# The seam behind a scan: pools per k tile, a split operand stored in DRAM, and a second partial sum through DRAM

## The chip, the cores and the metric

The kernel runs on one core of a Trainium2 chip. The core has five engines that each work through their own queue in order: TensorE (PE in the profile; its weight loads are PEld), VectorE (DVE), ScalarE (ACT), GpSimd (POOL) and SyncE (SP). SP, ACT and POOL also issue transfers (their queues are SPq, ACTq, POOLq). The metric is device time in microseconds of one execution; the time before is the median of three runs, 2103.34 us (2099.37 to 2106.05).

## The reference

One layer of a streaming encoder, in float32, for 1024 frames of width 1024:

```
u = rms_norm(x, ln1) * (1 + scale1) + shift1          # shift, scale, gate from silu(c) @ w_ada
gl, cb, cc, cx, z, xbc, dt = split(u @ w_in)
p_conv = (cb * causal_conv3(cc * cx)) @ w_conv_out
xs, bs, cs = split(silu(causal_conv4(xbc) + bias))
y = ssd_scan(xs * dt, dt * a, bs, cs) + d_skip * xs   # 32 heads in 8 groups, state 128
y = group_rms_norm(y * silu(z)) * ssm_norm_w
p_ssm = y @ w_ssm_out
x = x + gate1 * ((sigmoid(gl1) * p_conv + sigmoid(gl2) * p_ssm) @ w_o)
u2 = rms_norm(x, ln2) * (1 + scale2) + shift2
x = x + gate2 * (relu(u2 @ w_up) ** 2 @ w_down)
out = rms_norm(x, final_norm)
```

## The kernel before

Everything is held feature-major: a tile has 128 features on the partitions and 1024 frames, in two halves of 512. A matrix product is done in float32r from split operands: each operand is a high part (a cast on ACT) and a low part (operand minus high part, on DVE), and three matmuls (high x high, high x low, low x high) of 128x512 make one step over 128 inputs (`mm3`, lines 118 to 123). `proj` (line 125) does eight such steps for one output tile. `strassen_pair` (line 145) makes two output tiles at once with seven products instead of eight; its `wsplit` makes the four weight operands wa, w12, w34 and wb, each a whi and a wlo from the pool `weights`, which holds four of each in turn. A tile that is asked for while its place is still read waits for the last reader.

The stages, in order: the norm that makes u (`uh`, `ul`: high and low parts of eight k tiles, one pool `u`); a small projection for dt; the branch gates gl; z (eight pairs); the conv branch (for f0 = 0, 2, 4, 6: a v pair for f0, a v pair for f0+1, a y pair for both); the xBC projections, group by group (two x tiles, B, C), with the scan of the group before woven in; then the seam, where u is no longer needed and the conv output projection `wco` starts, with the scan of the last group woven in; then the SSD output projection `wso` in four quarters b = 0 to 3 of four k tiles each, the projection `wo`, and the MLP.

What the change touches, in the kernel before:

- 32 gemvs (line 319, a DVE instruction each, over 128x1024 weights that POOL loads) make the columns of the later modulation. They use one buffer `wv` (line 572) and stand in the gl and z stages: 4 with each gl pair from f = 12 on, 3 with each z pair.
- The conv branch writes each finished y tile (`glt`) to DRAM (`yc_d`, one float32 tile, line 662, ACT's queue). At the seam SP loads it into `ccs` (line 850, three buffers), and ACT and DVE split it into `ys` (`split`, line 108), one of eight tiles of the pool `yy`, which takes the place of `u`.
- `xbc_tile` (line 707) takes its weights from `load_w_acc` (line 99): the high part by a cast, the low part as the raw weights times -1 on ACT, and then a transfer on POOL's queue that adds the raw weights in DRAM. It copies the projection from PSUM to a padded tile `raw` and makes the tap sum `cacc` from PSUM.
- In `wso`, quarter 0 copies its sums from PSUM to `gt` and stores them to DRAM (`s_d`); quarter 1 loads them into slots and adds; quarters 2 and 3 add on in the slots. `finish` (line 806) makes a group's sum of squares, and `rstd` (line 822) the reciprocal roots of four groups, through DRAM (`ssq_d`, `rst_d`); the y tiles of a quarter are loaded (`yr`, two buffers, on SP), multiplied by the broadcast roots (`rb`, one buffer) on DVE and split into `ys`. `finish` of the last group stands at quarter 0, f = 2, `rstd(1)` at quarter 0, f = 5; quarters 2 and 3 need its result.

The order on each engine is not the order of the text: a scheduler places the instructions by an estimate of their times, and the priority follows the text.

Of the kernel before, what the change touches and what calls it, by code (L numbers as in the profile page):

```python
# [8 lines left out]
F32 = mybir.dt.float32  # L9
# [29 lines left out]
def hybrid_trunk(tc, xT, par, hrows, crow, wada1, wadak, wada2, win, wdt, wco, wso, wo, wup, wdt_, wdn, out):  # L39
# [43 lines left out]
    yc_d = dp.tile([8, P, T], F32, name="yc_d")  # L83
# [170 lines left out]
    up = tc.alloc_tile_pool(name="u", bufs=1, side="right")  # L254
    uh = [[up.tile([P, H], F32R, name=f"uh{k}{h}") for h in (0, 1)] for k in range(KT)]
    ul = [[up.tile([P, H], F32R, name=f"ul{k}{h}") for h in (0, 1)] for k in range(KT)]
# [284 lines left out]
    p0d = tc.alloc_tile_pool(name="p0d", bufs=1, reuse_waits="tile")
    wdr = p0d.tile([P, KT, NH], F32, name="wdr")
# [19 lines left out]

    p0d.release()
# [3 lines left out]
    gem = iter(range(32))  # L567

    def gemvs(n):
        for _, i in zip(range(n), gem):  # L570
            w_ = pe1.tile([P, T + 32], F32, name="wv", bufs=1)[:, 0:T]
            pool.dma_start(w_, wada2[i])  # L572
            gemv(w_, 16 + i)

# [28 lines left out]
    for f in range(8, 16, 2):  # L603
        ts_ = [glp.tile([P, T], F32, name="glt") for _ in (0, 1)]

        def gl_ev(i, h, src):
            act.activation(ts_[i][:, hs[h]], src, AF.Tanh, scale=0.5)

        if f == 10:
            dt_chain()  # L610
        elif f > 10:
            gemvs(4)
        strassen_pair(pe1, win[f], win[f + 1], X, gl_ev)
        for i in (0, 1):
            act.dma_start(gl_d[f + i], ts_[i])
    for g in range(NG):
        ts_ = [glp.tile([P, T], F32, name="glt") for _ in (0, 1)]

        def z_ev(i, h, src):
            t = ts_[i][:, hs[h]]  # L620
            act.activation(t, src, AF.Tanh, scale=0.5)
            stt(t, t, 1.0, src, ALU.add, ALU.mult)

        gemvs(3)
        strassen_pair(pe1, win[gtile(g) + 4], win[gtile(g) + 5], X, z_ev)
        for i in (0, 1):
            act.dma_start(z_d[2 * g + i], ts_[i])
# [9 lines left out]
    for f0 in range(0, 8, 2):  # L637
# [23 lines left out]
        for i in (0, 1):  # L661
            act.dma_start(yc_d[f0 + i], ys_[i])
# [33 lines left out]
    pcf = tc.alloc_tile_pool(name="pcf", bufs=2, reuse_waits="tile")  # L696
# [4 lines left out]
    padded = [p2t.tile([P, T + 3], F32, name=f"raw{i}", bufs=1) for i in (0, 1)]  # L701
# [4 lines left out]
    def xbc_tile(win_i, ci, dst):  # L706
        ps = proj(load_w_acc(win[win_i]), uh, ul)
# [4 lines left out]
        for h in (0, 1):  # L712
            act.activation(a[:, hs[h]], ps[h], AF.Identity, bias=hb[:, ci:ci + 1], scale=hw[:, 4 * ci + 3:4 * ci + 4])  # L713
# [5 lines left out]
    def proj_group(g):  # L719
# [7 lines left out]
        xbc_tile(b + 2, 16 + g, bf)  # L727
        xbc_tile(b + 3, 24 + g, cf)
# [126 lines left out]
    pcf.release()  # L855
# [4 lines left out]
    for f in range(8):  # L860
        drive(gen)
        gt = gp.tile([P, T], F32, name="gt")
        sp.dma_start(gt, gl_d[f])
        ps = proj(load_w(wco[f]), ych, ycl)
        for h in (0, 1):
            stt(gt[:, hs[h]], gt[:, hs[h]], 1.0, ps[h], ALU.add, ALU.mult)
        act.dma_start(at_d[f], gt)
    prev = drive(gen)
# [5 lines left out]
    for b in range(4):  # L874
        yh, yl = [], []
        for k in range(4):
# [7 lines left out]
            ys = yy.tile([P, 2, T], F32R, name="ys")  # L884
# [3 lines left out]
        if b == 1:  # L888
# [4 lines left out]
        for f in range(8):  # L893
            if f % 2 == 0:
                w = load_w(wso[b, f // 2])
            if b == 0:
                if f == 2:
                    finish(prev, last_mm[0])
                if f == 5:
                    rstd(1)  # L900
                gt = gp.tile([P, T], F32, name="gt")
                ps = proj(w, yh, yl, nk=4, base=(f % 2) * 512)
                for h in (0, 1):
                    act.copy(gt[:, hs[h]], ps[h])
# [9 lines left out]
            for h in (0, 1):  # L914
                if b == 1:
# [18 lines left out]
    yy.release()  # L934
# [283 lines left out]
```

## Time and profile before

| | |
|---|---|
| median of three runs | 2103.34 us |
| profiled execution | 2105.2 us |
| its span, first to last instruction | 2103.4 us |
| mean granted TensorE clock | 0.992 |
| TensorE busy | 2072.5 us (99%) |
| VectorE busy | 1473.1 us (70%) |
| ScalarE busy | 963.0 us (46%) |
| GpSimd busy | 182.6 us (9%) |
| conv branch | about 371 to 597 us |
| seam: last scan product, first conv output matmul | 1061.69 us, 1066.10 us |

In a row of the timeline stand the start, the duration, the engine, the line of the kernel, the operation and `out<-in`, and in brackets the idle time of the engine before it and what ended that. In a row of the waits of TensorE stand the total, the number of times and the longest. In a row of the windows stand the length, then for PE, PEld, DVE, ACT and POOL the busy time and the number of instructions, then the granted clock, the share of DMA time and GB/s.

### The profile page before, as it was taken

How to read it: one execution, taken by the hardware profiler on the slowest of the kernel's cores; microseconds unless marked ns; L12 is line 12 of the kernel's file. 1: busy time of each engine (PE TensorE's matmuls, PEld its weight loads, DVE VectorE, ACT ScalarE, POOL GpSimd, SP SyncE). 2: the span in 40 equal slices, each digit the busy share in tenths (PEclk: the TensorE clock that was granted, in tenths of full speed). 3: DMA queues.
4: the chain of work that ended last, by engine and by line, in shares of the span. 5: the costliest groups of instructions: out<-in, count | busy, mean ns of one | idle time of the engine just before them, and what ended most of it. 6: DMA issues, size and time to landing. Idle time of an engine off the chain costs nothing.

```text
span 2103.4 us, 26276 instructions
## 1 busy us (share of the span) xinstructions
PE 2072.5 (99%) x9760; PEld 1698.4 (81%) x9760; DVE 1473.1 (70%) x2310; ACT 963.0 (46%) x1600; POOL 182.6 (9%) x251
## 2 busy tenths in 40 slices
PE   8999999999999999999999999999999999999997
PEld 6878877888888888887878788888888888888887
DVE  8757777776637778877796748745866665658775
ACT  4433232332246768676564531224554454544432
POOL 0000000000000000000000000012000001232213
PEclk8999999999999999999999999999999999999998
DMA  8315645222274555555366676453144347988932
GB/s 327 106 64 187 203 161 194 87 70 74 77 202 111 123 123 136 140 142 137 99 207 219 213 282 198 167 194 118 61 165 165 150 157 268 304 239 254 284 75 81
DMA packets 139666, 345.16 MB, mean 164 GB/s; under 512 B 13153, under 2 KB 48353, under 8 KB 138002
## 3 DMA queue, kind: packets, MB, share of 16 engines
q1 hardware_dynamic: 98258, 200.14, 29.8%
q0 software_dynamic: 27856, 107.49, 18.0%
q10 hardware_dynamic: 13424, 35.85, 4.4%
q8 instruction: 77, 1.26, 0.2%
q14 instruction: 51, 0.42, 0.1%
HBM read 270.88 MB, written 72.55 MB: 163 GB/s over the span
## 4 chain that ended last, share of the span: by engine, by line
PE 87%; issue 8%; DMA 2%; DVE 1%; POOL 1%; ACT 0%; SPq 0%; DVEq 0%; POOLq 0%; ACTq 0%
PE mm L154 25%; PE mm L121 13%; PE mm L123 13%; PE mm L120 13%; PE mm L1111 11%; PE B L761 2%; PE mm L398 2%; PE B L766 2%; PE C L783 1%; PE sx L398 1%; PE st L398 1%; DMA wraw<-in_win 1%; POOL wv L572 1%; PE A L738 1%; DMA x<-in_xT 1%
## 5 line engine op out<-in xcount | busy, mean ns | idle before, releaser
L154 PE MATMUL mm<-t,whi 128*128 128x512 f32 x1104 | 340.9, 391 | 4.6 <-DVE cq L44 4.6
L154 PEld LDWEIGHTS mm<-t,whi 128*128 128x128 f32 x1104 | 207.6, 188 | 49.7 <-DVE cq L44 6.7
L154 PE MATMUL mm<-t,wlo 128*128 128x512 f32 x552 | 214.9, 390 | 0.0
L1111 PE MATMUL mm<-op,whi 128*128 128x512 f32 x672 | 207.0, 389 | 0.0
L121 PE MATMUL mm<-ul,whi 128*128 128x512 f32 x512 | 203.7, 398 | 0.0
L120 PE MATMUL mm<-uh,whi 128*128 128x512 f32 x512 | 203.3, 397 | 0.0
L44 DVE TENSOR_TENSOR wlo<-s,whi 128x1024 fp32r<-128x1024 f32 (+1 forms) x124 | 124.0, 1012 | 63.5 <-ACT whi L159 62.6
L123 PE MATMUL mm<-uh,wlo 128*128 128x512 f32 x512 | 162.3, 395 | 0.0
L44 DVE TENSOR_TENSOR wlo<-wraw,whi 128x1024 fp32r<-128x1024 f32 (+1 forms) x132 | 141.1, 1069 | 22.8 <-ACT whi L94 16.1
L120 PE MATMUL mm<-ys,whi 128*128 128x512 f32 x384 | 148.5, 394 | 3.7 <-ACT ys L109 3.7
L121 PE MATMUL mm<-ys,whi 128*128 128x512 f32 x384 | 148.8, 394 | 0.6 <-DVE ys L44 0.6
L47 DVE SCALAR_TENSOR_TENSOR cacc<-raw,hw,cacc 128x1024 f32<-128x1024 f32 x96 | 122.8, 1279 | 37.7 <-ACT cacc L713 37.0
L1111 PEld LDWEIGHTS mm<-op,whi 128*128 128x128 f32 x672 | 126.1, 188 | 26.2
L154 PE MATMUL mm<-s,whi 128*128 128x512 f32 x448 | 138.0, 389 | 0.7 <-ACT cu L177 0.7
L159 ACT CAST whi<-wraw 128x1024 fp32r<-128x1024 f32 x76 | 63.5, 836 | 157.8 <-PE mm L154 128.5
L1111 PE MATMUL mm<-op,wlo 128*128 128x512 f32 x336 | 130.7, 389 | 0.0
L755 ACT ACTIVATE seg<-acb,acum 128x128 f32<-128x128 f32 x256 | 81.9, 395 | 106.6 <-PE B L761 101.5
L47 DVE SCALAR_TENSOR_TENSOR y<-mm,mcol,y 128x512 f32<-128x512 f32 (+1 forms) x100 | 69.3, 704 | 78.1 <-PE mm L1111 41.3
L94 ACT CAST whi<-wraw 128x1024 fp32r<-128x1024 f32 x52 | 54.6, 1052 | 149.2 <-PE mm L121 127.0
L123 PE MATMUL mm<-ys,wlo 128*128 128x512 f32 x384 | 122.6, 394 | 0.0
L159 ACT CAST whi<-s 128x1024 fp32r<-128x1024 f32 x76 | 79.7, 1050 | 91.4 <-PE mm L154 85.3
L154 PEld LDWEIGHTS mm<-t,wlo 128*128 128x128 f32 x552 | 103.9, 188 | 21.7
(309 smaller groups left out, 4575.0 us busy)
## 6 DMA issues: line engine op xcount, KB each, us to landing
wraw<-in_win SPq DMA_DIRECT2D x83, 512.0 KB
dr<-in_wdt_ SPq DMA_DIRECT2D x108, 256.0 KB
op_d<-hp POOLq DMA_DIRECT2D x12, 1792.0 KB, 6.4
hr<-op_d POOLq DMA_DIRECT2D x42, 512.0 KB, 5.9
wv<-in_wada POOLq DMA_DIRECT2D x32, 512.0 KB, 3.8
wlo<-in_win POOLq DMA_DIRECT2D x32, 512.0 KB, 7.1
acb<-ac_d SPq DMA_DIRECT2D x64, 256.0 KB
wraw<-in_wup SPq DMA_DIRECT2D x32, 512.0 KB
```

What stands on the lines that cost most here:

```text
L44: return eng.tensor_tensor(out=o, in0=a, in1=b, op=op)
L47: return dve.scalar_tensor_tensor(out=o, in0=a, scalar=s, in1=b, op0=op0, op1=op1)
L94: act.copy(hi, raw)
L120: pe.matmul(o, lhsT=wh, rhs=h_, start=start, stop=False)
L121: pe.matmul(o, lhsT=wh, rhs=l_, start=False, stop=False)
L123: last_mm[0] = pe.matmul(o, lhsT=wl, rhs=h_, start=False, stop=stop)
L154: last_mm[0] = pe.matmul(o, lhsT=l_[:, s_], rhs=r_, start=first and k == j == 0, stop=k == 3 and j == 2, skip_group_check=True)
L159: act.copy(hi, src)
L398: pe.matmul(sps[f, h], lhsT=w_[f][:, j * P:j * P + P], rhs=v_[j][h], start=j == i == 0, stop=j == KT - 1 and i == 2, skip_group_check=True)
L755: act.activation(seg[:, r, :], acb[:, r, :], AF.Relu, bias=acum[:, c, hd:hd + 1], scale=-1.0)
L761: pe.matmul(Bk[o:o + 64, P * (r // 2):P * (r // 2) + P], lhsT=xd[:, r, :], rhs=seg[:, r, :], start=True, stop=True, skip_group_check=True)
L1111: pe.matmul(o, lhsT=l_[:, c_], rhs=t[:, r_, k, :], start=first and k == j == 0, stop=k == 3 and j == 2, skip_group_check=True)
```

## The change

- Gemvs: ten of the 32 go ahead of the dt projection into a pool `p0g` of three buffers; the other 22 stay in the gl and z stages, 3 and 2 per pair.
- u: one pool per k tile (`u0` to `u7`), and one pool per `ys` tile on the same memory, so that each y tile waits only for the last reader of its own k tile.
- Conv branch: each finished y tile is split there, into a `whi` and a `wlo` of the weight pool, and both parts are stored on POOL's queue; `yc_d` holds both. At the seam POOL loads both parts into `ys` with one transfer of 1 MB; `ccs` and its split are gone.
- xBC: `cacc` comes from the padded tile in one pass instead of from PSUM in two; the padding is wider.
- `staggered`: the B and C projections of the last group run against each other, shifted by four k tiles, and so do the first two conv output tiles.
- SSD projection: quarter 1 loads quarter 0's sums, adds on DVE and stores again; quarter 2 takes them into the slots. `finish` of the last group and `rstd(1)` move to quarter 1, f = 0 and f = 3, and the scan's pools are released at quarter 2.

```diff
-    yc_d = dp.tile([8, P, T], F32, name="yc_d")
+    yc_d = dp.tile([8, P, 2, T], F32R, name="yc_d")
+    def staggered(ws, xh, xl, done):
+        ps = [[mm.tile([P, H], F32, name="mm") for _ in hs] for _ in ws]
+        for i, k in [(0, k) for k in range(4)] + [(i, k + 4 - 4 * i) for k in range(4) for i in (0, 1)] + [(1, k) for k in range(4, KT)]:
+            c_ = slice(k * P, k * P + P)
+            mm3(ps[i], ws[i][0][:, c_], ws[i][1][:, c_], xh[k], xl[k], k == 0, k == KT - 1)
+            if k == KT - 1:
+                done(i, ps[i])
...
+    for k in range(KT):
+        up = tc.alloc_tile_pool(name=f"u{k}", bufs=1, side="right")
...
+    p0g = tc.alloc_tile_pool(name="p0g", bufs=1, reuse_waits="tile")
+    gemvs(10, p0g, 3)
...
-            gemvs(4)
+            gemvs(3, pe1)
...
-        gemvs(3)
+        gemvs(2, pe1)
...
         for i in (0, 1):
-            act.dma_start(yc_d[f0 + i], ys_[i])
+            hl = [wp.tile([P, T], F32R, name=n) for n in ("whi", "wlo")]
+            split(*hl, ys_[i])
+            for j in (0, 1):
+                pool.dma_start(yc_d[f0 + i][:, j, :], hl[j])
...
-        for h in (0, 1):
-            act.activation(a[:, hs[h]], ps[h], AF.Identity, bias=hb[:, ci:ci + 1], scale=hw[:, 4 * ci + 3:4 * ci + 4])
+        act.activation(a, raw[:, 3:3 + T], AF.Identity, bias=hb[:, ci:ci + 1], scale=hw[:, 4 * ci + 3:4 * ci + 4])
...
+        ws = [load_w_acc(win[b + i]) for i in (2, 3)]
+        staggered(ws, uh, ul, lambda i, ps: xbc_evac(ps, 16 + 8 * i + g, (bf, cf)[i]))
...
+    yys = [tc.alloc_tile_pool(name=f"yy{f}", bufs=1, side="right", reuse_waits="tile") for f in range(8)]
...
-        ccs = pcf.tile([P, T], F32, name="ccs", bufs=3)
-        sp.dma_start(ccs, yc_d[f])
-        y = yy.tile([P, 2, T], F32R, name="ys")
-        split(y[:, 0, :], y[:, 1, :], ccs)
+        y = next(yring).tile([P, 2, T], F32R, name="ys")
+        pool.dma_start(y, yc_d[f])
...
+    staggered([load_w(wco[f]) for f in (0, 1)], ych, ycl, gated)
...
-        if b == 1:
+        if b == 2:
             for p_ in (psC, psB, psA, p2, p2g[1], p2g[0]):
                 p_.release()
...
-            if b == 0:
-                if f == 2:
+            if b < 2:
+                if (b, f) == (1, 0):
                     finish(prev, last_mm[0])
-                if f == 5:
+                if (b, f) == (1, 3):
                     rstd(1)
                 gt = gp.tile([P, T], F32, name="gt")
+                if b == 1:
+                    sp.dma_start(gt, s_d[f])
                 ps = proj(w, yh, yl, nk=4, base=(f % 2) * 512)
                 for h in (0, 1):
-                    act.copy(gt[:, hs[h]], ps[h])
+                    if b == 0:
+                        act.copy(gt[:, hs[h]], ps[h])
+                    else:
+                        tt(gt[:, hs[h]], ps[h], gt[:, hs[h]], ALU.add)
                 act.dma_start(s_d[f], gt)
```

Three places in the built order. The first is ACT at the end of the first y pair of the conv branch (f0 = 0) and the start of the next v pair; before:

```order
L633 ACTIVATE glt<-wv,prm 128x1024
L159 CAST whi<-wraw 128x1024
L159 CAST whi<-s_3249 128x1024
L159 CAST whi<-s_3250 128x1024
L159 CAST whi<-wraw 128x512
L662 DMA yc_d<-glt 128x1024
L177 COPY cu<-mm 128x512
L662 DMA yc_d<-glt 128x1024
```

and now:

```order
L647 ACTIVATE glt<-wv,prm 128x1024
L109 CAST whi<-glt 128x1024 x2
L167 CAST whi<-wraw 128x1024
L167 CAST whi<-s_3284 128x1024
L167 CAST whi<-s_3285 128x1024
L167 CAST whi<-wraw 128x512
L185 COPY cu<-mm 128x512
```

The two casts of the finished y tiles (`glt`) now stand ahead of the four casts of the next pair's weights, where before those four stood ahead of y's stores.

The second is POOL around the end of the conv branch (`raw` is the padded tile, `wlo<-in_win` the accumulating load of a low part); before:

```order
L642 MEMSET wv 128x2 x8
L105 DMA wlo<-in_win 128x1024 x3
L703 MEMSET raw_4478 128x3
L703 MEMSET raw_4479 128x3
L105 DMA wlo<-in_win 128x1024 x10
```

and now:

```order
L656 MEMSET wv 128x2
L719 MEMSET raw_4540 128x3
L719 MEMSET raw_4541 128x3
L679 DMA yc_d<-whi 128x1024
L679 DMA yc_d<-wlo 128x1024
L679 DMA yc_d<-whi 128x1024
L679 DMA yc_d<-wlo 128x1024
L105 DMA wlo<-in_win 128x1024 x13
```

All accumulating loads of the xBC stage now stand behind the four stores of the last y pair.

The third is DVE from the reciprocal roots (`sq`, `ym`, `yt`, small `yr`) to the operands of the SSD projection's quarter 2 (large `yr`, `ys`); before, with quarter 1's additions into the slots `s`:

```order
L50 TENSOR_SCALAR yr<-yr 32x128
L44 TENSOR_TENSOR wlo<-wraw,whi 128x1024
L44 TENSOR_TENSOR s_10382<-mm,s_10382 128x512
L44 TENSOR_TENSOR s_10385<-mm,s_10385 128x512
L44 TENSOR_TENSOR s_10414<-mm,s_10414 128x512
L44 TENSOR_TENSOR s_10417<-mm,s_10417 128x512
L44 TENSOR_TENSOR wlo<-wraw,whi 128x1024
L47 SCALAR_TENSOR_TENSOR yr<-yr,prm,rb 128x1024 x2
L44 TENSOR_TENSOR ys<-yr,ys 128x1024
```

and now, with quarter 1's additions into `gt`:

```order
L50 TENSOR_SCALAR yr<-yr 32x128
L44 TENSOR_TENSOR gt<-mm,gt 128x512 x4
L47 SCALAR_TENSOR_TENSOR yr<-yr,prm,rb 128x1024 x2
L44 TENSOR_TENSOR wlo<-wraw,whi 128x1024
L44 TENSOR_TENSOR ys<-yr,ys 128x1024 x2
L47 SCALAR_TENSOR_TENSOR yr<-yr,prm,rb 128x1024 x2
L44 TENSOR_TENSOR ys<-yr,ys 128x1024 x2
L47 SCALAR_TENSOR_TENSOR yr<-yr,prm,rb 128x1024 x2
L44 TENSOR_TENSOR s_10719<-mm,s_10719 128x512
```

Before, the first additions behind the roots are those of quarter 1's first tiles, and the operands of quarter 2 are spread over that quarter; now the four additions are the last of quarter 1, and the operands of quarter 2 come right behind them, with the first addition of quarter 2 itself (`s_10719`) behind those of quarter 3's first y.

More of the change, by code (lines that the diff above doesn't have):

```diff
@@ L252, in hybrid_trunk @@
     z2 = d0.tile([P, NC_ * NH], F32, name="z2")
-    up = tc.alloc_tile_pool(name="u", bufs=1, side="right")
-    uh = [[up.tile([P, H], F32R, name=f"uh{k}{h}") for h in (0, 1)] for k in range(KT)]
-    ul = [[up.tile([P, H], F32R, name=f"ul{k}{h}") for h in (0, 1)] for k in range(KT)]
+    ups_, uh, ul = [], [], []
+    for k in range(KT):
+        up = tc.alloc_tile_pool(name=f"u{k}", bufs=1, side="right")
+        ups_.append(up)
+        for n, u_ in (("uh", uh), ("ul", ul)):
+            u_.append([up.tile([P, H], F32R, name=f"{n}{k}{h}") for h in (0, 1)])
     cbp = tc.alloc_tile_pool(name="cbp", bufs=1)
@@ L540, in hybrid_trunk, with gemvs @@
         xk[k].release()
+    gem = iter(range(32))
+    def gemvs(n, pl, bufs=1):
+        for _, i in zip(range(n), gem):
+            w_ = pl.tile([P, T + 32], F32, name="wv", bufs=bufs)[:, 0:T]
+            pool.dma_start(w_, wada2[i])
+            gemv(w_, 16 + i)
     p0d = tc.alloc_tile_pool(name="p0d", bufs=1, reuse_waits="tile")
+    p0g = tc.alloc_tile_pool(name="p0g", bufs=1, reuse_waits="tile")
+    gemvs(10, p0g, 3)
     wdr = p0d.tile([P, KT, NH], F32, name="wdr")
@@ L566, in hybrid_trunk @@
     pe1 = tc.alloc_tile_pool(name="pe1", bufs=2, reuse_waits="tile")
[L567 to L573, printed above, removed]
     def as3(a):
@@ L699, in hybrid_trunk @@
     psC = tc.alloc_tile_pool(name="psC", bufs=1, space=PSUM)
-    padded = [p2t.tile([P, T + 3], F32, name=f"raw{i}", bufs=1) for i in (0, 1)]
+    padded = [p2t.tile([P, T + 32], F32, name=f"raw{i}", bufs=1) for i in (0, 1)]
     for raw in padded:
@@ L726, in proj_group @@
         xbc_tile(b + 1, 2 * g + 1, xs[:, 1, :])
-        xbc_tile(b + 2, 16 + g, bf)
-        xbc_tile(b + 3, 24 + g, cf)
+        if g < NG - 1:
+            xbc_tile(b + 2, 16 + g, bf)
+            xbc_tile(b + 3, 24 + g, cf)
+            return xs, bf, cf
+        ws = [load_w_acc(win[b + i]) for i in (2, 3)]
+        staggered(ws, uh, ul, lambda i, ps: xbc_evac(ps, 16 + 8 * i + g, (bf, cf)[i]))
         return xs, bf, cf
@@ L859, in hybrid_trunk, with gated @@
     prev = None
-    for f in range(8):
-        drive(gen)
+    def gated(f, ps):
         gt = gp.tile([P, T], F32, name="gt")
         sp.dma_start(gt, gl_d[f])
-        ps = proj(load_w(wco[f]), ych, ycl)
         for h in (0, 1):
@@ L867, in hybrid_trunk @@
         act.dma_start(at_d[f], gt)
+    drive(gen)
+    staggered([load_w(wco[f]) for f in (0, 1)], ych, ycl, gated)
+    drive(gen)
+    for f in range(2, 8):
+        drive(gen)
+        gated(f, proj(load_w(wco[f]), ych, ycl))
     prev = drive(gen)
@@ L883, in hybrid_trunk @@
             stt(yr, yr, prm[:, SNW + kk:SNW + kk + 1], rb_, ALU.mult, ALU.mult)
-            ys = yy.tile([P, 2, T], F32R, name="ys")
+            ys = next(yring).tile([P, 2, T], F32R, name="ys")
             split(ys[:, 0, :], ys[:, 1, :], yr)
@@ L933, in hybrid_trunk @@
     gp.release()
-    yy.release()
+    for p_ in reversed(yys):
+        p_.release()
     d0.release()
```

13 lines of the change are left out of this document (7 added, 6 removed).

## The prediction, as it was put on record

> **What bounds the kernel now.** I read the page first: busy time by engine and the chain of waits, then what TensorE waited for.
>
> ```profile
> span 2103.4 us, 26276 instructions
> PE 2072.5 (99%) x9760; PEld 1698.4 (81%) x9760; DVE 1473.1 (70%) x2310; ACT 963.0 (46%) x1600; POOL 182.6 (9%) x251
> ...
> PE 87%; issue 8%; DMA 2%; DVE 1%; POOL 1%; ACT 0%; SPq 0%; DVEq 0%; POOLq 0%; ACTq 0%
> ...
> PE mm L154 <- DVE cq L44: 4.6, 4, 2.6
> PE mm L120 <- ACT ys L109: 3.7, 1, 3.7
> PE mm L121 <- DVE ys L44: 0.6, 1, 0.6
> ```
>
> TensorE is busy 99% of the span and the change leaves its matmuls as they are. So only its gaps count: 30.9 us now (2103.4 - 2072.5), of which the rows above, in the stages that the change touches, hold 8.9. Whatever the change wins lies in these; what it loses are new gaps. After a gap comes the clock:
>
> ```profile
> 286.44 0.87 PE L154 MATMUL mm<-t,whi 128*128 128x512 f32 x2 [2.56 <-DVE cq L44]
> ...
> 286.00:288.00 2.00, 1.56 (x5) 1.23 (x6) 1.07 (x2) 1.58 (x3) 0.53 (x1) 0.72 0.16 16
> 288.00:290.00 2.00, 2.00 (x6) 1.61 (x5) 1.82 (x2) 1.41 (x2) 0.00 (x0) 0.50 0.65 246
> 290.00:292.00 2.00, 2.00 (x9) 1.60 (x8) 1.91 (x4) 0.00 (x0) 0.32 (x1) 0.93 0.00 0
> ...
> 1066.10 1.22 PE L120 MATMUL mm<-ys,whi 128*128 128x512 f32 x2 [3.70 <-ACT ys L109]
> 1067.96 1.22 PE L121 MATMUL mm<-ys,whi 128*128 128x512 f32 x2 [0.63 <-DVE ys L44]
> ...
> 1066.00:1068.00 2.00, 1.26 (x3) 0.55 (x3) 2.00 (x5) 2.00 (x5) 0.00 (x0) 0.50 0.95 221
> 1068.00:1070.00 2.00, 2.00 (x5) 1.61 (x6) 2.00 (x2) 2.00 (x6) 0.00 (x0) 0.50 0.73 246
> 1070.00:1072.00 2.00, 2.00 (x7) 1.50 (x6) 2.00 (x4) 1.99 (x6) 0.00 (x0) 0.52 0.58 199
> ```
>
> The last column but two is the granted clock. A gap of 2.56 us is followed by a clock of 0.72, 0.50, 0.93 over three windows of 2 us: 2 x (0.28 + 0.50 + 0.07) = 1.7 us more. At the seam 3.70 + 0.63 us of waiting and about 5.3 us at half clock (2.6 lost) make 6.9; counted by matmuls (15 in 6 us) it is 6.2. I take 6.5 for the seam and 1.7 for the clock after any gap of 2.5 to 5 us. The Trainium skill (TensorE: Matmul & The Clock Gate, Part 1) lets the clock drop only after an idle window of about 3.4 us; here 2.56 us sufficed, so the trace decides, and for gaps near 5 us the two agree.
>
> **Seam: won.** y arrives split; the load of each y needs only its own u pool. In the order the C projection (i=0) ends early and the last projection is interleaved with conv-output matmuls, so neither the 3.70 nor the 0.63 remains: -6.5 us. Eight casts and eight subtractions leave ACT and DVE, and the conv bias pass reads one tile instead of two PSUM banks; both engines are off the path there, so 0. New are 8 loads of 1 MB on POOL's queue. By the order the first is released 48 big and 21 small matmuls before the seam (about 13 us) and the eighth y is first read 70 big and 19 small after it (about 18 us).
>
> ```profile
> op_d<-hp POOLq DMA_DIRECT2D x12, 1792.0 KB, 6.4
> wv<-in_wada POOLq DMA_DIRECT2D x32, 512.0 KB, 3.8
> wlo<-in_win POOLq DMA_DIRECT2D x32, 512.0 KB, 7.1
> ```
>
> At 1792 KB in 6.4 us, 8 MB take 30 us against 31 available, beside other loads. I charge 2 us (0 if the queue keeps up, 8 if it runs a quarter slower). The Trainium skill (SBUF — State Buffer, "Who interferes with whom") says that DVE in its two-port mode holds up descriptors that GpSimd writes; no row here shows such a hold, and by that rule the loads would come later still.
>
> **Gemvs: a little won.** The four waits for cq are 0.79, 2.56, 0.36 and 0.90 us, each at a DVE queue held by a gemv whose weights had not landed. Ten of 32 gemvs move into DVE's idle stretch after the dt weights:
>
> ```profile
> 134.21 1.29 DVE L44 TENSOR_TENSOR s<-wraw 128x512 f32<-128x512 f32 x2 [21.93 <-PE st L558]
> 345.89 0.50 PE L154 MATMUL mm<-t,whi 128*128 128x512 f32 x1 [0.36 <-DVE cq L44]
> 366.12 0.73 PE L154 MATMUL mm<-t,whi 128*128 128x512 f32 x2 [0.90 <-DVE cq L44]
> ```
>
> With three buffers each gemv costs at most (3.8 + 1.3 + 0.5) / 3 = 1.9 us there, the ten 19 of 21.9 us. The other 22 stand where the first 22 stood, so the first two waits stay and the last two go: -1.3 us (-6.3 if all four and the clock go; +1 if the tenth is late).
>
> **Conv branch: a new gap at the end of each y pair.** This is the main loss. Before, ACT casts the next pair's first weights a whole pair ahead and TensorE steps over without a gap:
>
> ```profile
> 414.74 1.05 ACT L159 CAST whi<-wraw 128x1024 fp32r<-128x1024 f32 x1 [3.37 <-PE mm L154]
> ...
> 425.42 0.39 PE L154 MATMUL mm<-t,wlo 128*128 128x512 f32 x1
> 425.64 0.39 PE L154 MATMUL mm<-uh,whi 128*128 128x512 f32 x1
> 425.87 0.39 PE L154 MATMUL mm<-ul,whi 128*128 128x512 f32 x1
> ```
>
> (One matmul in 0.225 us.) After, y's two tiles take turns in the same ring of four whi and wlo, and the order puts both casts of y ahead of the next pair's first cast on ACT. The second y cast needs the last product. Prices come from the last y pair; T = 596.78 is the start of its last matmul:
>
> ```profile
> 596.78 0.40 PE L154 MATMUL mm<-t,wlo 128*128 128x512 f32 x1
> ...
> 597.21 0.69 DVE L44 TENSOR_TENSOR cu<-mm,cu 128x512 f32<-128x512 f32 x1 [1.31 <-PE mm L154]
> 597.94 0.69 DVE L44 TENSOR_TENSOR glt<-cu,glt 128x512 f32<-128x512 f32 x1
> ...
> 597.02 1.05 ACT L102 CAST whi<-wraw 128x1024 fp32r<-128x1024 f32 x1 [0.71 <-PE mm L154]
> 597.97 1.05 ACT L104 ACTIVATE wlo<-wraw 128x1024 fp32r<-128x1024 f32 x1
> ...
> 588.41 0.87 POOL L105 DMA_DIRECT2D wlo<-in_win  x1 [21.31 <-ACT wlo L104]
> ...
> L44 DVE TENSOR_TENSOR wlo<-wraw,whi 128x1024 fp32r<-128x1024 f32 x94 | 115.2, 1226 | 22.8 <-ACT whi L94 16.1 <-ACT whi L159 5.6
> ```
>
> cu is added at T+0.43; then DVE runs the first tile's low part (1.23, new, ahead in its queue), and the product with glt ends at T+3.0. ACT casts the second tile (1.05) to T+4.1 and the next weights (0.95 later) to T+5.05. TensorE resumes at T+5.1 instead of T+0.23: 4.9 us, with the clock 6.6. Three such ends (f0 = 0, 2, 4) give **+19.8** (14.7 without any clock loss; 22.5 if the low parts and stores add 0.9 each).
>
> The fourth end runs into the first xBC projection. Its weights' low part is made by ACT (x -1) and an accumulating load on POOL. Before, that load is issued at 588.41, 8.6 us before TensorE steps over (597.0). In the new order ACT does the second y cast (T+4.1), two weight casts (T+6.0), then the product with -1 (T+7.0); POOL's accumulate stands behind four y stores and goes out at about T+7. With 7.1 us to land it is there at T+14.1. Till then TensorE has eight matmuls and the decay sums, some 3.3 us (8 x 0.225, and 1.5 as an estimate for the small products). 14.1 - 0.2 - 3.3 = 10.6, with the clock **+12.3** (9 by the 3.8 us of the plain load above; 16 if four stores of 512 KB delay it by half their 7.5 us at 280 GB/s).
>
> **SSD projection: the second quarter.** Copying or adding a PSUM half costs alike on ACT or DVE, and 8 more loads and stores of 512 KB are not waited for. But the last group's square sums and their rsqrt move from the first quarter into the second, and the third needs the result. By the order, 81 matmuls (18.4 us) stand between the last square-sum matmul and the end E of the second quarter. The chain's prices:
>
> ```profile
> 1220.80 0.24 ACTq L820 DMA_DIRECT2D ssq_d<-row  x1
> 1221.94 0.32 SPq L824 DMA_DIRECT2D sq<-ssq_d  x1
> ...
> 1227.73 11.73 SPq L917 DMA_DIRECT2D s<-s_d  x11
> 1228.40 0.33 ACTq L827 DMA_DIRECT2D rst_d<-yr  x1
> ...
> L47 DVE SCALAR_TENSOR_TENSOR yr<-yr,prm,rb 128x1024 f32<-128x1024 f32 x16 | 20.2, 1280 | 4.6 <-DMA yr<-y_d 4.6
> L109 ACT CAST ys<-yr 128x1024 fp32r<-128x1024 f32 x16 | 16.7, 1053 | 24.7 <-DVE yr L47 17.8 <-PE mm L123 6.5
> ```
>
> Row to rst_d took 7.6 us; with the row copy, two additions and a split between them some 12; issue and landing of the broadcast (1.1 + 3.8 by the gemv's load) make 17 to 19, about E. On DVE the first product with it stands behind the last two additions, which wait for E: E+1.4, +1.28, +1.05 for the cast: TensorE starts the third quarter at E+4. Worse is what follows: yr has two buffers, so the third and fourth y are loaded only after the first two are split (E+6), behind the loads of the sums on SP, and these took 1.07 us per 256 KB. 4.5 MB queue there from about E+1: 16 us at 280 GB/s, 19 by that row. With its product and cast the third y is ready at E+14 to E+20, TensorE having run 24 of 48 matmuls by E+11; the other 24, and then the quarter's first additions behind the next yr on DVE, whose load again waits for a split, take some 9 us more. So 48 matmuls end at E+23 to E+29 instead of E+11. I take **+15** (9 if the loads land in 3.8 us; 20 with a full queue and the clock).
>
> **Sum** on the profiled execution's 2105.2 us (span 2103.4): -6.5 + 2 - 1.3 + 19.8 + 12.3 + 15 = +41.3, or 2146.5. The median of the runs is 1.9 us lower than that execution: 2144.6, I say 2145. All low bounds together: -6.5 - 6.3 + 14.7 + 9 + 9 = +20, 2123; all high: -6.5 + 8 + 1 + 22.5 + 16 + 20 = +61, 2164.
>
> **Rivals.**
> 1. The third quarter's operands are in time: the broadcast lands early and the loads of the sums, of which eight tiles wait on nothing, are through before E. For it: in the trace DMA is only in part busy and the chain took 7.6 us. Against it: the two DVE additions ahead in the queue. Price -15 + 4: 2134, and with a fourth end at its low bound 2130.
> 2. POOL's queue binds at the seam: it now carries 8 MB within 31 us. If a load takes 5 us instead of 3.7, the last y comes at 27 instead of 18 us, and the seam loses 9 + 1.7 instead of 2: 2154.
> 3. Faster: the pair ends are not late. The mechanism is that the y casts and low parts run in the gaps of ACT and DVE (54% and 30% idle) before TensorE is through, and the next weights with them; it decides from 1.5 us of cover per end. Then the seam and all four cq waits with their clock are won and nothing is lost: 2103.3 - 6.5 - 6.3 = 2090. Against it stands the written order: the second cast needs the last product, so at least 0.69 + 0.69 + 2.0 us pass.
> 4. It does nothing measurable: seam and gemvs (-7.8 to -12.8) against three ends at 3.4 us without loss of clock (+10.2), the fourth and the third quarter hidden: about 2103.
>
> **Chances.** Forecast 0.55, rival 1 0.22, rival 2 0.10, rival 3 0.08, rival 4 0.05. A measurement of this kernel can tell 0.3%, 6.3 us: slower 0.87, same 0.05, faster 0.08. The range 2115 to 2163 leaves out rivals 3 and 4 and the far ends; the forecast's own is 2130 to 2160.
>
> **What would show it.** In the profile after: a wait of TensorE for ACT's whi of 4 to 5 us, three times, between 420 and 560 us, with a clock near 0.5 behind each; a wait of about 10 us for the accumulated wlo near 600; no wait of 3.7 us for ys at the seam; waits for ys of 4 us and more at the third quarter. I am wrong if TensorE stays above 98% busy between 420 and 620 us, or if what waits there is something other than the first weights of a pair.

## The result, and the profile after

The changed kernel takes 2162.44 us (median of four runs, 2160.07 to 2165.67) against 2102.29 us (four runs, 2099.37 to 2106.05) of the kernel before beside it: a ratio of 1.0286, 95% interval 1.0264 to 1.0308. It is slower by 60 us where 42 were forecast; 2162 lies inside the range, at its upper edge. The profiled execution took 2165.67 us, 3.2 above its median. The forecast's own range, 2130 to 2160, was just missed. The runs below were timed at other times than the changed kernel; the kernel before beside them took 2105.17 to 2105.56 us, so a gain "against the changed kernel" is good to some 3 us.

The page of the changed kernel, its span and busy times, and what TensorE waited for (total, times, longest):

```profile
span 2163.9 us, 26306 instructions
PE 2093.7 (97%) x9760; PEld 1711.2 (79%) x9760; DVE 1473.6 (68%) x2310; ACT 959.8 (44%) x1568; POOL 194.7 (9%) x275
```

```profile
PE mm L162 <- ACT whi L167: 13.8, 3, 4.6
PE mm L120 <- ACT ys L109: 13.6, 2, 8.3
PE mm L123 <- DMA wlo<-in_win: 10.4, 1, 10.4
...
PE mm L162 <- DVE cq L44: 2.6, 3, 1.3
PE mm L1143 <- DVE y L47: 2.4, 2, 1.6
PE st L692 <- DVE strict L50: 2.2, 1, 2.2
```

TensorE's gaps grew from 30.9 to 70.2 us (2163.9 - 2093.7), and its busy time by 21.2 us for the same 9760 matmuls: 17.4 of these are work at a lower clock (29.0 us lost to it by the clock records of the trace instead of 11.7). The first three rows are the three places that the prediction named. The wait of 3.70 us for ys at the seam is gone: both waits of row two lie in the third quarter of the SSD projection (below). The waits for cq are 2.6 instead of 4.6 us; run 7, which leaves the gemvs where they were, shows 1.1, so this fall isn't shown to be the gemvs' doing.

**A y pair's end.** The timeline of the changed kernel at the first of them (start, duration, engine, line, operation):

```profile
424.27 0.39 PE L162 MATMUL mm<-t,wlo 128*128 128x512 f32 x1
424.70 0.69 DVE L44 TENSOR_TENSOR cu<-mm,cu 128x512 f32<-128x512 f32 x1 [1.30 <-PE mm L162]
425.31 1.21 DVE L44 TENSOR_TENSOR wlo<-glt,whi 128x1024 fp32r<-128x1024 f32 x1
426.44 0.69 DVE L44 TENSOR_TENSOR glt<-cu,glt 128x512 f32<-128x512 f32 x1
427.21 1.04 ACT L109 CAST whi<-glt 128x1024 fp32r<-128x1024 f32 x1 [2.68 <-DVE glt L44]
428.17 1.04 ACT L167 CAST whi<-wraw 128x1024 fp32r<-128x1024 f32 x1
429.26 0.80 PE L162 MATMUL mm<-uh,whi 128*128 128x512 f32 x1 [4.59 <-ACT whi L167]
...
617.57 0.40 PE L162 MATMUL mm<-t,wlo 128*128 128x512 f32 x1
```

Its windows (length; busy time of PE, PEld, DVE, ACT, POOL; granted clock; DMA share; GB/s):

```profile
426.00:428.00 2.00, 0.00 (x0) 0.00 (x0) 1.12 (x2) 0.79 (x1) 0.53 (x1) 0.73 0.73 264
428.00:430.00 2.00, 0.74 (x2) 0.50 (x2) 1.71 (x2) 2.00 (x3) 0.72 (x2) 0.50 0.88 320
430.00:432.00 2.00, 2.00 (x6) 1.49 (x5) 2.00 (x3) 1.54 (x3) 0.35 (x1) 0.50 1.03 352
432.00:434.00 2.00, 2.00 (x6) 1.51 (x5) 1.12 (x2) 0.17 (x1) 0.00 (x0) 0.56 0.90 254
```

ACT holds the cast of the next weights (428.17) behind the cast of the second y tile (427.21), which waits for the last product of the pair. From its last matmul to the first of the next pair TensorE takes 4.99 us. From the last matmul of the first y pair to that of the fourth it is now 617.57 - 424.27 = 193.30 us; before it was 596.78 - 425.42 = 171.36. The three ends cost 21.94 us, or 7.3 each: 4.8 from one matmul to the next (4.99 instead of 0.23) and 2.3, 2.6 and 2.8 of clock, which is 0.50 already while TensorE still waits and stays there for 4.5 us of work at the first end (the clock records of the trace have 0.50 from 426.92 to 433.75).

**The fourth end.** The timeline of the changed kernel from there on, and its windows:

```profile
618.13 0.53 POOL L679 DMA_DIRECT2D yc_d<-whi  x1 [0.88 <-ACT whi L109]
...
620.62 0.70 PE L692 MATMUL st<-z,strict 128*128 128x256 f32 x2 [2.22 <-DVE strict L50]
...
623.06 0.53 POOL L679 DMA_DIRECT2D yc_d<-wlo  x1 [0.73 <-DVE wlo L44]
...
623.30 2.00 ACT L104 ACTIVATE wlo<-wraw 128x1024 fp32r<-128x1024 f32 x2
...
624.65 1.82 POOL L105 DMA_DIRECT2D wlo<-in_win  x2 [1.06 <-ACT wlo L104]
...
636.94 1.22 PE L123 MATMUL mm<-uh,wlo 128*128 128x512 f32 x2 [10.43 <-DMA wlo<-in_win]
```

```profile
622.00:624.00 2.00, 2.00 (x8) 1.40 (x7) 0.76 (x1) 2.00 (x3) 0.86 (x2) 0.50 1.06 401
624.00:626.00 2.00, 1.81 (x7) 1.14 (x6) 0.40 (x1) 2.00 (x5) 1.29 (x2) 0.78 1.09 412
626.00:628.00 2.00, 0.51 (x4) 0.20 (x3) 0.03 (x1) 1.24 (x2) 0.48 (x1) 1.00 1.11 412
...
634.00:636.00 2.00, 0.00 (x0) 0.00 (x0) 0.00 (x0) 0.00 (x0) 0.85 (x1) 0.50 1.07 272
...
640.00:642.00 2.00, 2.00 (x6) 1.52 (x5) 0.00 (x0) 0.00 (x0) 0.00 (x0) 0.51 1.03 273
```

The accumulating load goes out 7.1 us after T = 617.57 (the start of the pair's last matmul), as forecast, but its first use comes 12.3 us later (636.94 - 624.65), while the DMA share is over 1.0: four stores of y, other accumulating loads and the loads of raw weights share it. Waiting 2.22 + 10.43, and about 4 us lost to the clock (1.0 and 0.4 in the first two windows shown, 2.5 between 636.9 and 642): some 17 us. Counted from T to the 48th matmul of the first xBC tile it is 30.68 us instead of 13.13: 17.6 more.

The four stores of y are not shown to make the load slow. In the kernel before, the loads issued just before and after its T (at 596.61 and 599.32) landed after 10.9 and 12.2 us (its view of transfers in short windows around these two):

```profile
wlo<-in_win POOLq DMA_DIRECT2D x1, 512.0 KB, 10.9
...
wlo<-in_win POOLq DMA_DIRECT2D x1, 512.0 KB, 12.2
```

Only the first load, issued at 588.41, was quick there (it landed after 6.4 us), and it is the one that TensorE needs first. In the changed kernel the first load goes out inside the crowded stretch. No run keeps this late load without the stores.

**The third quarter.** Its timeline in the changed kernel:

```profile
1308.89 0.32 SPq L906 DMA_DIRECT2D rb<-rst_d  x1
...
1311.30 0.61 PE L123 MATMUL mm<-ys,wlo 128*128 128x512 f32 x2
...
1317.16 2.07 PE L120 MATMUL mm<-ys,whi 128*128 128x512 f32 x4 [5.25 <-ACT ys L109]
...
1323.58 0.85 SPq L908 DMA_DIRECT2D yr<-y_d  x2
...
1333.11 2.08 PE L120 MATMUL mm<-ys,whi 128*128 128x512 f32 x4 [8.31 <-ACT ys L109]
...
1342.40 0.50 PE L120 MATMUL mm<-ys,whi 128*128 128x512 f32 x1 [1.14 <-DVE s L44]
```

The second quarter ends at E = 1311.75. The third's first 48 matmuls run in 10.9 us without gaps; here the 49th starts at 1342.40: 30.65 - 10.9 = 19.75 us lost. The whole quarter takes 63.4 us instead of 43.5. The third and fourth y tile are asked for only at 1323.58, behind the loads of the sums.

### The profile page after: what moved, and what is told of

Its sections match the earlier page's. It is cut to its first block, busy times and chain, and to the rows that moved or that the text cites. A ratio compares the mean times of both kernels' runs of the same rounds, so it can differ in the third digit from the quotient of the medians.

```text
span 2163.9 us, 26306 instructions
## 1 busy us (share of the span) xinstructions
PE 2093.7 (97%) x9760; PEld 1711.2 (79%) x9760; DVE 1473.6 (68%) x2310; ACT 959.8 (44%) x1568; POOL 194.7 (9%) x275
## 4 chain that ended last, share of the span: by engine, by line
PE 67%; issue 5%; DMA 4%; DVE 4%; POOL 0%; ACT 0%; SPq 0%; DVEq 0%; POOLq 0%; ACTq 0%
PE mm L162 16%; PE mm L123 12%; PE mm L120 12%; PE mm L121 12%; PE mm L1143 8%; PE B L782 2%; PE B L787 1%; DMA yr<-y_d 1%; DMA dr<-in_wdt_ 1%; PE C L804 1%; DVE wlo L44 1%; PE A L759 1%; DMA s<-s_d 1%; DVE s L44 1%; DMA wlo<-in_win 1%
## 5 line engine op out<-in xcount | busy, mean ns | idle before, releaser
L120 PE MATMUL mm<-uh,whi 128*128 128x512 f32 x512 | 203.9, 398 | 0.0
L162 PE MATMUL mm<-uh,whi 128*128 128x512 f32 x288 | 115.4, 401 | 14.7 <-ACT whi L167 13.8
L167 ACT CAST whi<-wraw 128x1024 fp32r<-128x1024 f32 x76 | 63.5, 836 | 145.9 <-PE mm L162 126.2
L123 PE MATMUL mm<-ys,wlo 128*128 128x512 f32 x384 | 127.5, 394 | 0.0
L123 PEld LDWEIGHTS mm<-uh,wlo 128*128 128x128 f32 x512 | 96.2, 189 | 29.9 <-DMA wlo<-in_win 10.7
```

The lines of the kernel that those rows point to most:

```text
L120: pe.matmul(o, lhsT=wh, rhs=h_, start=start, stop=False)
L123: last_mm[0] = pe.matmul(o, lhsT=wl, rhs=h_, start=False, stop=stop)
L162: last_mm[0] = pe.matmul(o, lhsT=l_[:, s_], rhs=r_, start=first and k == j == 0, stop=k == 3 and j == 2, skip_group_check=True)
L167: act.copy(hi, src)
```

## The experiments

The theory: three orders make the loss, one in each stage, and undoing one of them gives its part back. The rivals are named with each run.

**1. The roots in time.** The reciprocal roots are made for group pairs; those of groups 4 and 5 at the last scan (c = 6, g = 7), so that only groups 6 and 7 stay behind the second quarter's third tile.

```diff
             if c == 6 and g == 5:
-                rstd(0)
+                rstd(0, 4)
+            if c == 6 and g == 7:
+                rstd(4, 2)
...
                 if (b, f) == (1, 3):
-                    rstd(1)
+                    rstd(6, 2)
```

> The changed kernel, but the reciprocal roots of groups 4 and 5 are made during the last scan and only those of groups 6 and 7 in the second quarter. Theory (the third quarter waits for the roots, and its second pair of operands is queued behind them): the waits of 5.3, 8.3 and 1.1 us for ys at the third quarter go, the 19.8 us that the quarter's start lost come back: about 2143 us. Rival (the SP queue is the cause, full of the loads of the sums, whatever the roots do): the 5.3 us go, the 8.3 us and most of the clock stay: about 2154 us.

Measured 2142.72 us (2141.09 to 2143.89), ratio to before 1.0177 [1.0162, 1.0192]: 19.7 us won against the changed kernel. In its waits both rows for ys are gone and the other two places stay:

```profile
PE mm L162 <- ACT whi L167: 13.8, 3, 4.6
PE mm L123 <- DMA wlo<-in_win: 8.7, 1, 8.7
```

In its profile the third quarter takes 43.5 us, as in the kernel before, so all of its 19.9 us are back. That the times differ by 19.7 as well is partly luck: other stages of this profile are longer (4.7 us more between the first group's xBC tiles and the end of the second quarter) and shorter (3.2 before the conv branch, in code that is the same), and by the ratios the gain would be 22.9 us. The third quarter's loss is the lateness of the roots, not the place of the loads of the sums by itself: SP still carries the same loads. With the roots in time, though, the quarter's y tiles are asked for from 1263.7 to 1276.5, ahead of the loads of the sums (from 1312.7), so how much of the wait of 8.31 us those loads made once the roots were late is not told apart.

**2. y not split in the conv branch.** The float32 tile is stored on ACT's queue as before; at the seam POOL loads it into half of `ys`, where it is split in place. Pools per k tile and all else stay as changed.

```diff
-            hl = [wp.tile([P, T], F32R, name=n) for n in ("whi", "wlo")]
-            split(*hl, ys_[i])
-            for j in (0, 1):
-                pool.dma_start(yc_d[f0 + i][:, j, :], hl[j])
+            act.dma_start(yc_d[f0 + i], ys_[i])
...
-        pool.dma_start(y, yc_d[f])
+        raw = y[:, 1, :].bitcast(F32)
+        pool.dma_start(raw, yc_d[f])
+        split(y[:, 0, :], y[:, 1, :], raw)
```

> The changed kernel, but y of the conv branch is stored unsplit on ACT's queue as before; at the seam each y is loaded into the low half of its place and split there, the low part in place. Theory (y's casts stand ahead of the next pair's weights, y's stores ahead of the first accumulating loads): three waits of 4.6 us and the one of 10.4 us go, with their clock 40 us: 2122 to 2126 us, the seam still without a wait of 1 us or more, since the pools per k tile give the splits 13 us of lead. Rival (it is the split at the seam that cost the wait there): the seam's 6.5 us come back: about 2130 us. Rival (the fourth end is not the stores but the order of POOL and ACT around the decay sums): 18 us stay: about 2141 us.

Measured 2116.04 us (2112.26 to 2119.42), ratio 1.0053 [1.0036, 1.0070]: 46.4 us won, 6 more than the most that the theory said (2122). Its conv branch has no wait for whi or wlo, and its seam has none although the split is back there. By the rows the three pair ends and the fourth end are back at the length of before, which is 39.5 us won. The waits of the SSD projection changed too (timeline of this run, a wait in the third quarter and one in the fourth):

```profile
1280.50 2.08 PE L120 MATMUL mm<-ys,whi 128*128 128x512 f32 x4 [8.19 <-ACT ys L109]
...
1341.40 0.79 PE L120 MATMUL mm<-ys,whi 128*128 128x512 f32 x1 [3.79 <-DVE gt L47]
```

The third quarter takes 54.4 us instead of 63.4, but the fourth, which had no wait, 50.1 instead of 43.5: 2.4 us won in both together. The rest isn't resolved; the four runs spread over 7 us. Splitting at the seam costs TensorE no wait in the changed kernel. That the pools per k tile make this so is not shown: `staggered` came with them, and no run has one without the other.

**3. Both.** The first two edits together.

> The two edits together: y stored unsplit and split in place at the seam, roots in pairs. Theory (the three places are separate and account for nearly all): 2162.4 - 19.8 - 40 = 2103 us, 2098 to 2106; below the kernel before only by what the seam (6.5) and the gemvs (1.1) won and later stages have not given back. Rival (the places share one cause, such as DMA traffic): the gains do not add, 2115 us or more.

Measured 2098.18 us (six runs, 2096.93 to 2099.41), ratio 0.9964 [0.9952, 0.9976]: faster than both kernels, by 7.4 us than the one before in the same call (2105.56). The two gains alone, 19.7 + 46.4, would have given 2096.3, so they add up within 2 us (within some 4 by the ratios). What is left of its waits in the stages of the change:

```profile
PE mm L162 <- ACT cu L185: 1.6, 2, 0.9
...
PE mm L162 <- DVE cq L44: 1.3, 2, 0.7
...
PE C L837 <- DVE state L44: 0.5, 1, 0.5
```

**4. The second cast written later.** y's parts are split and stored in the conv branch, but for f0 = 0, 2, 4 the split of the second tile stands in the text behind the next pair's weight splits.

```diff
         w12 = wsplit(s12)
+        for h_ in held:
+            h_()
...
+            if i == 1 and f0 < 6:
+                held = [lambda f=f0 + 1, y=ys_[1]: put(f, y)]
+            else:
+                put(f0 + i, ys_[i])
```

> The changed kernel; only the split of the second y tile of the pairs f0 = 0, 2, 4 is written after the next pair's first two weights instead of before them. Same ring of four, same stores. Theory (the place of that cast in ACT's queue makes the wait): the three waits of 4.6 us shrink to at most 1.2 us and the clock stays at 1: 2162.4 - 18 to 22 = 2141 to 2144 us. Rival (the ring of four shared with y's stores makes it: a place comes free only when a store has landed): the wait moves to the next weights, at most half is won: 2152 us or more.

Measured 2142.54 us (2141.64 to 2146.26), ratio 1.0180 [1.0165, 1.0195]. The timeline of this run at two of the ends, and the windows at the first:

```profile
421.83 0.50 PE L162 MATMUL mm<-uh,whi 128*128 128x512 f32 x1 [0.87 <-ACT whi L167]
...
422.78 1.19 PE L162 MATMUL mm<-t,whi 128*128 128x512 f32 x4 [0.21 <-ACT whi L167]
...
424.61 0.50 PE L162 MATMUL mm<-uh,wlo 128*128 128x512 f32 x1 [0.65 <-DVE wlo L44]
...
481.54 0.50 PE L162 MATMUL mm<-uh,whi 128*128 128x512 f32 x1 [0.87 <-ACT whi L167]
```

```profile
422.00:424.00 2.00, 1.75 (x6) 0.80 (x6) 2.00 (x3) 1.19 (x2) 0.53 (x1) 1.00 0.72 262
424.00:426.00 2.00, 1.39 (x6) 1.17 (x7) 2.00 (x3) 1.53 (x2) 0.53 (x1) 1.00 0.83 283
```

The gap of 4.59 us becomes three of 0.87, 0.21 and 0.65, and the clock stays at 1.00. From one end to the next it is now 481.54 - 421.83 = 59.71 us instead of 64.15 (429.26 to 493.41 in the changed kernel): 4.4 us per end. From the last matmul of the first y pair to that of the fourth it takes 599.67 - 420.57 = 179.10 us instead of 193.30, so the edit gives back 14.2 us of the ends' 21.9. The forecast was met, but not by the ends alone: the first y pair also ended 3.7 us earlier (420.57 against 424.27), in a part that this edit does not touch, and smaller differences lie behind. That the order of two casts on ACT makes the gap is shown; the work is the same.

**5. Quarter 1 back in the slots.** The third run's kernel with the second quarter's sums taken into the slots as before, `finish` and the last roots back in quarter 0, and the scan's pools released at quarter 1.

```diff
-        if b == 2:
+        if b == 1:
             for p_ in (psC, psB, psA, p2, p2g[1], p2g[0]):
                 p_.release()
...
-            if b < 2:
-                if (b, f) == (1, 0):
+            if b == 0:
+                if f == 2:
                     finish(prev, last_mm[0])
```

> The version with y unsplit and the roots in pairs, but the second quarter of the SSD projection adds in the slots as in the kernel before, with the last group's square sums and roots written in the first quarter again. Theory (with the seam rebuilt the last scan ends about a quarter later, so the slots, which take the scan's memory, come too late for the second quarter): TensorE waits at the second quarter, 4 us or more above the 2098 us of that version. Rival (the detour through DRAM buys nothing): 2096 to 2100 us.

Measured 2110.86 us (seven runs, 2108.72 to 2115.96), ratio 1.0034 [1.0022, 1.0047], 12.7 us above the third run's kernel. The timeline shows a new gap at the second quarter:

```profile
1248.15 0.80 PE L120 MATMUL mm<-ys,whi 128*128 128x512 f32 x1 [8.28 <-DVE s L44]
```

With the rebuilt seam the slots are not ready when the second quarter starts (its first matmul is at 1225.8, the first load into a slot goes out at 1242.8; in the kernel before these were 1233.6 and 1225.2), so the detour through DRAM is worth 12.7 us there, as long as the roots come in time.

**6. The gemvs alone.** The kernel before with only the move of ten gemvs to the pool `p0g`.

```diff
+    p0g = tc.alloc_tile_pool(name="p0g", bufs=1, reuse_waits="tile")
+    gemvs(10, p0g, 3)
...
-            gemvs(4)
+            gemvs(3, pe1)
```

> The kernel before with the gemv part alone: ten gemvs ahead of the dt projection, 3 and 2 per pair behind. Theory (two of four waits for cq go, the others shift): 1 to 3 us below the kernel before, not told from it. Rival (all four go with their clock): 6 us below.

Measured 2105.25 us (eleven runs) against 2105.47 (18 runs): ratio 0.9998 [0.9988, 1.0008]. The waits for cq fell from 4.6 to 0.6 us in its profile, which would be 4 us and the clock behind them, yet nothing is left of it in the time; the interval allows up to 2.5 us. Its profile has waits for y of 3.8 us in the down projection that the profile of before has not, and from the projection `wo` to the end it takes 745.8 us instead of 739.2. Whether these are connected is not known. Nor is the fall of the waits for cq shown to be the move's doing: run 7, with the gemvs in their old place, has 1.1 us of them.

**7. The split store alone.** The kernel before with y split and stored in the conv branch and loaded on POOL at the seam, into the one pool `yy`: no pools per k tile, nothing else.

```diff
-            act.dma_start(yc_d[f0 + i], ys_[i])
+            hl = [wp.tile([P, T], F32R, name=n) for n in ("whi", "wlo")]
+            split(*hl, ys_[i])
+            for j in (0, 1):
+                pool.dma_start(yc_d[f0 + i][:, j, :], hl[j])
```

> The kernel before with the split of y in the conv branch alone (high and low part stored on POOL, loaded at the seam by one transfer of 1 MB each into the pool that takes the place of all of u). Theory: the four ends of the y pairs cost 40 us as in the changed kernel; at the seam the loads wait for all of u and 8 MB take some 30 us, against 11 us for the first tile's matmuls and what of the scan stands between: the seam gets worse by 8 to 16 us: 2150 to 2162 us. Rival (the casts made the seam's wait, the pool did not): the seam's 6.5 us are won: about 2139 us.

Measured 2139.09 us (2135.43 to 2142.04), ratio 1.0161 [1.0142, 1.0180]. The theory missed: it expected the seam to get worse by 8 to 16 us, since no load can start before all of u is free. Its timeline at the seam, and the loads on its page (KB each, median us from issue to landing):

```profile
1098.65 0.47 PE L120 MATMUL mm<-ys,whi 128*128 128x512 f32 x1 [3.19 <-DMA ys<-yc_d]
```

```profile
ys<-yc_d POOLq DMA_DIRECT2D x8, 1024.0 KB, 15.8
```

TensorE waits 3.19 us there, for the first load, less than the 3.70 + 0.63 of before, though a load takes 15.8 us in the median instead of 8.9 in the changed kernel (all eight go out within 4.0 us); the other seven came in time. Its conv branch has the same three waits of 4.6 us, and one of 8.8 us for wlo. So the split in the conv branch alone costs 33.6 us. Removed from the changed kernel it gave 46.4. In the rows of the pair ends and the fourth end the two agree: 22.3 + 15.1 = 37.4 us here, 21.9 + 17.6 = 39.5 there. Of the rest, 3.0 us are won here between the first group's xBC tiles and the end of the second quarter, and there 2.4 in that stretch and 2.4 in the SSD projection's third and fourth quarter (second run); what is left lies in stages that neither edit touches.

**8. The stores on ACT's queue.** The changed kernel with the stores of y's parts issued by ACT instead of POOL.

```diff
-                pool.dma_start(yc_d[f0 + i][:, j, :], hl[j])
+                act.dma_start(yc_d[f0 + i][:, j, :].bitcast(F32), hl[j].bitcast(F32))
```

> The changed kernel with the stores of y's parts on ACT's queue instead of POOL's. Theory (the first accumulating load is late because ACT makes its input late and DMA is full): three waits of 4.6 us stay, the wait for wlo stays at 8 to 11 us: 2158 to 2164 us. Rival (POOL's queue makes it late, four stores ahead): the wait for wlo falls to about 5 us: about 2156 us or less.

Measured 2162.29 us (two runs), ratio 1.0274 [1.0253, 1.0296]; the waits are those of the changed kernel, with 8.8 us for wlo, as in the runs that keep the stores on POOL (8.7 in run 1, 8.5 in run 4). The load goes out 7.6 us after T, no earlier than the 7.1 of the changed kernel. POOL's queue is not what holds the accumulating load: that it stood behind four stores there cost nothing that is seen.

**9. The first low parts on DVE.** The first four xBC tiles make their low parts by a subtraction, without the accumulating load.

```diff
-        xbc_evac(proj(load_w_acc(win[win_i]), uh, ul), ci, dst)
+        xbc_evac(proj((load_w if win_i < 44 else load_w_acc)(win[win_i]), uh, ul), ci, dst)
```

> The changed kernel with one edit: the first four xBC tiles (two x tiles, B and C of the first group) make their low parts as every other stage does, by a subtraction on DVE, and not by the product with -1 on ACT and the accumulating load; the other 28 keep the load. Theory: of the fourth end's 18 us some 10.4 are the wait for the accumulated load, which lands 12.3 us after it is issued among four stores of 512 KB; a subtraction on DVE needs 1.2 us after ACT's cast, so that wait falls to 0 to 2 us, the half clock behind it with it: 2148 to 2153 us. Rival: what is late is the raw weights or ACT's cast itself, in a full DMA stage, so the subtraction is late as well and a wait of 6 us or more for DVE's wlo takes its place: 2157 to 2162 us.

Measured 2153.58 us (2153.15 to 2156.23), ratio 1.0228 [1.0209, 1.0247]: 8.9 us won, 0.6 us short of the theory's range. The timeline of this run has the low part on DVE in time, and no gap before its first use:

```profile
620.61 0.70 PE L692 MATMUL st<-z,strict 128*128 128x256 f32 x2 [2.22 <-DVE strict L50]
...
622.67 2.35 DVE L44 TENSOR_TENSOR wlo<-wraw,whi 128x1024 fp32r<-128x1024 f32 x2
...
625.58 0.62 PE L123 MATMUL mm<-uh,wlo 128*128 128x512 f32 x2
```

The rival, raw weights or casts that come late themselves, falls. From T to the 48th matmul of the first xBC tile it takes 17.4 us, against 30.7 in the changed kernel and 13.1 before: 13.3 of the fourth end's 17.6 us are won there, and 4.2 remain, the 2.22 for `strict`, which stands on DVE behind y's low part and last product, and the clock behind that gap. Of the 13.3, 8.9 reach the time; in this profile the third quarter takes 3.7 us more than in the changed kernel's, and the first quarter 2.4 more. Why is open.

**10. Three orders, the split kept.** Runs 1, 4 and 9 in one kernel.

> The changed kernel with three edits and y's split still in the conv branch: the roots over group pairs (first experiment, -19.7 us against the changed kernel), the cast of the second y tile behind the next pair's first weights at three ends (fourth experiment, -19.9), and the low parts of the first four xBC tiles on DVE (the experiment beside this one, forecast -10 to -14). Theory: the three losses lie in three stages and add up, so undoing them adds up too: 2108 to 2114 us, still 3 us and more above the kernel before, since the fourth end keeps its late casts. Rival: the stages share engines and transfers, and one stage's relief becomes the next one's wait: 2120 us or more. If it comes out at 2103 or less, the split in the conv branch costs nothing in itself, and only its place in the order did.

Measured 2116.29 us (six runs, 2113.43 to 2121.18), ratio 1.0050 [1.0032, 1.0067]. The gains alone, 19.7 + 19.9 + 8.9, would have given 2113.9: the time is 2.4 us above that (7.8 by the ratios). It lies between the two forecasts, 2.3 us above the theory's range and 3.7 below the rival's: most of the gains add up, not all. It stays 18.1 us above the third run's kernel, which does not split y in the conv branch. Its page:

```profile
PE 2077.5 (98%) x9760; PEld 1697.2 (80%) x9760; DVE 1477.3 (70%) x2326; ACT 957.1 (45%) x1564; POOL 191.2 (9%) x271
```

Against the third run's profile TensorE is busy 5.4 us more and idle 15.6 us more (40.1 against 24.5). Of the idle time 5.2 us are the small gaps at the three ends (3.3 for whi, 1.9 for wlo) and 2.2 the wait for `strict`; the rest is spread over small waits. By stages of the two profiles, 7.8 us more lie at the pair ends, 3.2 at the fourth end, 5.5 between the first group's xBC tiles and the end of the second quarter, and the rest before and behind, where the code is the same.

## Why the prediction was right, and where it was short

| term of the sum | predicted | measured |
|---|---|---|
| seam | -6.5 | no wait left there; -3.7 up to the end of the second quarter |
| loads of y at the seam | +2 | no wait for them |
| gemvs | -1.3 | nothing measurable alone (run 6); waits for cq 2.6 instead of 4.6, but 1.1 without the move (run 7) |
| three y pair ends | +19.8 | +21.9 |
| fourth end | +12.3 | +17.6 (14.9 to 15.9 in the profiles of runs 1, 4, 7 and 8) |
| third quarter | +15 | +19.9 (rows), all of it back in run 1's rows |
| elsewhere | 0 | +4.8 |

- **The direction and the three places** were right, and each by the step that was written: the cast of the next weights behind the second y cast (shown by run 4), the accumulated low part as the last operand at the fourth end (run 9), the roots as the start of the third quarter's delay (run 1). The forecast of 4.9 us per pair end came out as 4.8, the issue of the accumulating load at T + 7 as T + 7.1. The wait of 10.43 us for that load against the forecast 10.6 is luck: it came 5.3 us later than forecast (T + 19.4 instead of T + 14.1), and TensorE had 8.7 us to fill until then instead of 3.3, of them 2.22 the wait for `strict`, which the sum did not have, and the matmuls at half clock.
- **The three sizes were too small, for two reasons.** The clock: 1.7 us per gap was taken from a gap of 2.56 us; behind one of 4.6 it is 2.3 to 2.8. The transfers: 7.1 us for the accumulating load is the median over the whole stage; at this place, at a DMA share over 1.0, the first took 12.2 to 12.3, and two loads at the same place in the trace of before had taken 10.9 and 12.2. The median hid them. The third quarter was taken at +15 because the loads of the sums might land fast; they went as in the row of 1.07 us each, and the loss is the high end of 20 almost exactly.
- **The seam**'s waits are gone as forecast, and the +2 for POOL's loads was not needed: its 8 MB were in time. Rival 2, POOL's queue as the bound, is out by this. Of the 6.5 us, 3.7 are kept: from the end of the first group's xBC tiles to the end of the second quarter, 3312 matmuls in both, it takes 630.6 us instead of 634.4, with 1.1 us of new waits in the first quarter. What became of the other 1.7 us is not known.
- **Rivals 1, 3 and 4** are out by the waits: the third quarter's operands were not in time, and the pair ends were late. Most of the cover that rival 3 asked for was there once the second cast was placed later (run 4).
- **About 5 us lie outside the terms.** 21.9 + 17.6 + 19.9 - 3.7 is 55.7 of the 60.5 us between the two spans. From the projection `wo` to the end it takes 745.2 us instead of 739.2, in code that the change does not touch: two waits for y (2.4 us in all) and 3.4 us lost at a clock of 0.50 from 2123.3 to 2130.1, which follows no wait but 24 matmuls of a single column; the kernel before runs the same place at 1.00. The first y pair ends 1.1 us earlier. Run 6, as fast as the kernel before, takes 745.8 us there, and the other runs 740.8 to 744.4, so this is not a mark of the slower kernel; what makes the waits late is open.

## What to carry to other kernels

Work that is moved out of a crowded stage is not free in the quieter one: it stands in the in-order queue of an engine that prepares the next operands, and the second of two casts there waits for the last product of the stage. So before moving such work, find the next operand behind it on that engine, and write the late piece behind that operand; or leave it where it was, if another edit already removes the wait (here the pools per tile or the staggered order). And a landing time that is the median over a stage need not be that of the one transfer that counts: look that one up in the trace.

## What was not expected of the hardware

- One gap of 4.59 us was followed by 0.50 for 4.5 us of work (2.3 us lost); three gaps of 0.87, 0.21 and 0.65 us within 4 us left the clock at 1.00. Their sum is only 1.73 us, so whether it counts that the gap is in one piece is not shown. The Trainium skill (TensorE: Matmul & The Clock Gate, Part 1) has the clock fall after an idle window of about 3.4 us. The three short gaps agree with that. The gap of 2.56 us in the kernel before and that of 2.22 us at the fourth end, each followed by 0.50, do not, and the clock fell 2.3 us into the gap of 4.59 (424.66 to 426.92). Nor does the length of a gap decide alone: the same 2.22 us for `strict` left the clock at 1.00 in runs 4 and 10.
- An accumulating load of 512 KB landed after 12.2 us at a DMA share of 1.03 to 1.11, against a median of 7.1 on the page of before; at the same place the kernel before has 10.9 and 12.2, at a share of 1.00 to 1.10.
- Loads of 1 MB, eight of them issued within 4.0 us, took 15.8 us each in the median and left TensorE waiting 3.19 us at the old seam (run 7), less than the 4.33 us with the loads, cast and subtraction that they replaced.
